# Seven more products in seven parts in the second layer of a two-layer encoder trunk, and an earlier place for the sums that two of them read

## The chip, the cores and the metric

The kernel runs on one core of a Trainium2 chip. Its time is the device time of one execution in microseconds (us). On the core, TensorE (PE in the profile) multiplies matrices, VectorE (DVE), ScalarE (ACT) and GpSimd (POOL) work element by element, SyncE (SP) issues transfers, and 16 DMA engines carry them out. TensorE writes into eight banks of PSUM.

## What is computed

The trunk has two layers over 512 frames of width 1024, in float32. The reference, cut to what the change touches:

```python
for i in range(DEPTH):
    h = rmsnorm(x, norm1_g[i])
    z = h @ w_in[i] + b_in[i]
    _, _, mv, mo, mi, mf, rq, rk, rv, rg, gm, gr = split_cols(z)
    ...
    hm = from_chunks(hm)                       # matrix memory, 4 heads of 256
    y_m = (jax.nn.sigmoid(mo) * head_layernorm(hm, m_norm_g[i], M_HEADS))
    ...                                        # retention gives y_r
    merged = jax.nn.sigmoid(gm) * (y_m @ w_bm[i]) + jax.nn.sigmoid(gr) * (y_r @ w_br[i])
    x = x + merged @ w_out[i]

    h2 = rmsnorm(x, norm2_g[i])
    x = x + jnp.square(jax.nn.relu(h2 @ w_ff1[i] + b_ff1[i])) @ w_ff2[i] + b_ff2[i]
    ...
```

`mo` has 1024 columns, 256 for each of four heads; its sigmoid is the output gate of the matrix memory. `w_ff1` is 1024 x 4096, `w_ff2` 4096 x 1024: the two products of the channel mix.

## The kernel before

**Float32 by three products.** Every operand is split into a high part, rounded to the matmul's float32r, and a low part, the rest. `split` (L302) makes both: ScalarE copies the high part (L303), VectorE subtracts (L304). A product is high x high + high x low + low x high, so three matmuls for each block of 128 rows of the inner dimension.

**Units of weights.** The weights come as a list of units, made by `unit_list` (L171) in the order of use, and loaded through SP's queue by `fill_raws` (L397), at most four pieces ahead (`RAWS`) and one more in places. Each piece is split before use (`prep_next`, L425). Three kinds matter here:

- a `T8` unit is 1024 x 128 of weights, one piece. `t8` (L484) makes 24 matmuls of 512 columns into one bank.
- a `PAIR` unit gives two such tiles, 256 columns, in seven products instead of eight (Strassen's scheme in Winograd's form): `run_pair` (L512), with 12 matmuls of 256 columns for each of seven parts, 84 in all, where two `T8` units have 48 of 512. The weights are pieces A, B, C (1024 wide) and D (512 wide), seven blocks of 128 x 512. The order of parts is P1, P5, P6, P2, P3, P7; P4 is put off (`later`) and made inside the next unit, after its first four inner blocks (`t8`, L491), after its P5 (`run_pair`) or after the first block of an attention (`attend`, L838), by `flush` (L507). Three banks hold the parts; ScalarE and VectorE gather them into two tiles y (`pair_tiles`, L587, ScalarE for P1, P5, P6, P4 and VectorE for P2, P3, P7). When P4 has come, `consume` goes on with the two tiles; the second comes with its sign turned.
- a `V` unit is a quarter of the weights of a value tile (`values`, L783).

**Sums.** A product in seven parts needs sums of blocks on both sides. The sums of weights (t1, t3, t2, t4) are made by DMA from DRAM to DRAM, some copying and some adding, on POOL's queue: `step` (L354) issues one, and holds it until the latest matmul has run. For groups that `is_full` (L128) names, all four are made so, in eight steps for a product; for others VectorE forms the rest. `tick` and `pace` (L365, L369) say when: each unit adds credit by its time in `TIME`, times `SHARE`, or `LATER` from a unit in the first layer on, less what its loads cost; a step takes `STEP` of credit. The order of steps is that of `groups` (L147), and a load of a group may only be issued when its steps are (the assertion in `fill_raws`). The sums of activations are made by VectorE and ScalarE: `xs_sums` (L1228), four calls of eight VectorE and two ScalarE instructions for the normed input x of the layer, and `n2_sums` (L1457) for the channel mix. They use scratch tiles of 128 x 512 (`tmp`, six of them in this stage, `NTMP`).

**Order around the change.** In the stage of the matrix memory the program runs, for heads 0 to 3, the query and key tiles (`m_qk`), scores, attention (`m_attend`), the gates (`m_gates`, two `T8` units a head) and the way back to the transposed form (`m_back`, transposes on TensorE and a gating on VectorE). The values of heads two and three are made by `mv_vals(1, ...)`, four `V` units; a function `mid` given to it runs ahead of its third unit. A scheduler then puts the instructions of each engine in an order of its own, by their place in the program and the tiles they need; the order shown in the profile is its outcome.

In the channel mix `ff_order` (L79) gives the sequence: the tiles (0,0) to (0,3) of the first product (256 hidden columns each, `ff1`, L1477), then for each b from 0 to 2 the tile (b+1,0), four output products (b,0) to (b,3) (`ff2`, L1514, always in seven parts), and the tiles (b+1,1) to (b+1,3); then the last four output products. An output product (b,p) reads the four hidden tiles (b,0) to (b,3). After each hidden tile come the norm's factor (L1485), relu and square on ScalarE, then the hidden tile's own split and sums for the next product (`pair_quarters`, `pair_operand`). `FPAIRS` (L90) lists the (b,p) that are made by `PAIR` units, five in each layer.

The instructions' names in the profile: l1f13 is layer two's hidden tile (1,3), and its matmuls are l1f13a, b, c by bank when it is a product in seven parts and l1f when it is two plain tiles; l1o10 is the output product (1,0); l1hh and l1hl are the hidden operands' high and low parts; l1m2o is the output gate of head three (counted from nought, 2), l1bgm a branch gate, l1xsh and l1xsl the sums of normed x, wh and wl the weights' parts (with a letter for pieces of a `PAIR`), s29t a sum of weights.

Of the kernel before, what the change touches and what calls it, by code (L numbers as in the profile page):

```python
# [37 lines left out]
AF = mybir.ActivationFunctionType  # L38
# [23 lines left out]
SIGN = (1.0, -1.0)  # L62
# [24 lines left out]

FPAIRS = ((1, 1), (1, 3), (2, 1), (2, 3), (3, 1))  # L90


PRODUCTS = {"P1": ("A", 0, 0), "P5": ("A", 1, 4), "P2": ("B", 0, 2), "P6": ("B", 1, 5), "P3": ("C", 0, 6),
# [14 lines left out]
HALVES = [(WIDE[x][0], u) for x, u in TURNS]  # L108

SOON = ("w_in", 0, CGM + 2 * P)  # L110
STEP, SHARE, LATER = 1.13, 0.75, 0.73
TIME = {"PAIR": (9.9, 3.9), "WIDE": (5.45, 2.7), "FULL": (9.9, 5.0)}


# [12 lines left out]

def is_full(g):  # L128

    return is_gate(g) or g[0] > 0 and g[1][0] == "f"  # L130


def has_t2(g):
# [4 lines left out]
def is_gate(g):  # L138
    return g[1][:2] == "rw"
# [7 lines left out]
def groups():  # L147


    g = {}  # L150
    for i in range(L):
        def rqk(h):
            return [("w_in", 0, c + k * 256) for k in (h, h + 1) for c in (CRQ, CRK)]

        g[i, "rv0"] = [("w_in", 0, CRV)]
        g[i, "rqk0"] = rqk(0)
        g[i, "gm"] = [("w_in", 0, CGM + 256 * p) for p in (2, 3)]
        g[i, "rw0"] = [("w_in", 0, CRG)]
        g[i, "rv2"] = [("w_in", 0, CRV + 1024)]
        g[i, "rqk2"] = rqk(2)  # L160
        g[i, "rw2"] = [("w_in", 0, CRG + 1024)]
        g[i, "gr"] = [("w_in", 0, CGR + 256 * p) for p in range(4)]
        for b in range(4):
            f = [p for c, p in FPAIRS if c == b]
            if f:
                g[i, f"fp{b}"] = [("w_ff1", 0, b * 1024 + 256 * p) for p in f]
            g[i, f"ff{b}"] = [("w_ff2", b * 1024, 256 * p) for p in range(4)]
    return g


def unit_list(i):  # L171

    u = [("IF",)]

    def t8(w, col, row=0):
        u.append(("T8", w, row, col))

    def v(col):
        for k in range(4):
            u.append(("V", k, col))  # L180

    def pair(g, p):
        u.append(("PAIR", (i, g), p))

    def mqk(h):
        for d in range(2):
            t8("w_in", CQ + h * 256 + d * P)
        for d in range(2):
            t8("w_in", CK + h * 256 + d * P)

    def mo(h):
        for d in range(2):
            t8("w_in", CO + h * 256 + d * P)

    def rqk(h):
        for a in range(2):
            pair(f"rqk{h // 2 * 2}", h % 2 * 2 + a)

    def full(w, col=0, row=0, lo=0, hi=8):
        for c in range(lo, hi):  # L200
            t8(w, col + c * P, row)

    mqk(0)
    v(CV)
    full("w_in", CGM, 0, 0, 2)
    mqk(1)
    mo(0)
    full("w_in", CGM, 0, 2, 3)
    mqk(2)
    mo(1)  # L210
    v(CV + 512)
    mqk(3)
    mo(2)
    full("w_in", CGM, 0, 3, 4)
    mo(3)
    u.append(("WIDE", (i, "rv0"), 0))
    full("w_bm", 0, 0, 0, 4)
    rqk(0)
    for p in (2, 3):
        pair("gm", p - 2)  # L220
        full("w_bm", 0, 0, 2 * p, 2 * p + 2)
    rqk(1)
    u.append(("WIDE", (i, "rw0"), 0))
    u.append(("WIDE", (i, "rv2"), 0))
    rqk(2)
    full("w_br", 0, 0, 0, 4)
    rqk(3)
    full("w_br", 0, 0, 4, 8)
    u.append(("WIDE", (i, "rw2"), 0))
    for p in range(4):  # L230
        pair("gr", p)
        full("w_br", 0, 1024, 2 * p, 2 * p + 2)
    full("w_out")

    def pairs(seq):
        for kind, b, p in seq:
            if (b, p) in FPAIRS and kind == "f":
                pair(f"fp{b}", [q for c, q in FPAIRS if c == b].index(p))
            elif kind == "f":
                t8("w_ff1", b * 1024 + 256 * p)  # L240
                t8("w_ff1", b * 1024 + 256 * p + P)
            else:
                pair(f"ff{b}", p)

    pairs(ff_order()[0])
    u.append(("PE", 0))
    pairs(ff_order()[1])
    u.append(("PE", 1))
    full("w_pe_gate")
    return u  # L250


def build(ctx, tc, ins, out):
# [529 lines left out]
    def values(i, nm, act, rc, bv_ap, n_, mid=None):  # L783

        bvt = tmp(f"{nm}bv")
        (gp if nm == "l0m0" else nc.sync).dma_start(bvt, bv_ap)
        o = [ps(f"{nm}vp{j}") for j in range(NT)]
        for u in range(4):
            _, wh, wl = unit("V")
            if u == 1:  # L790
                flush()
            if u == 2 and mid:
                mid()
            for kk in range(2):
                k = 2 * u + kk
                s = slice(kk * T, (kk + 1) * T)
                for j in range(NT):
                    js = slice(j * P, (j + 1) * P)
                    te.matmul(o[j], act[0][k][:, js], wh[:, s], start=(k == 0), stop=False)
                    te.matmul(o[j], act[0][k][:, js], wl[:, s], start=False, stop=False)  # L800
                    cur["mm"] = te.matmul(o[j], act[1][k][:, js], wh[:, s], start=False, stop=(k == KT - 1))
                pace()
        vh = [cur["low"].tile([P, 576], F32R, name=f"{nm}vh{j}", tag="vh", bufs=NT) for j in range(NT)]
        vl = [cur["low"].tile([P, 576], F32R, name=f"{nm}vl{j}", tag="vl", bufs=NT) for j in range(NT)]
        for j in range(NT):
            rows_split_v(i, None, nm, n_, j, o[j], rc, bvt, vh[j], vl[j])
        return vh, vl
# [167 lines left out]
    for i in range(L):  # L975
# [125 lines left out]
        def m_gates(h, act, nrm):  # L1101
            return [gated(f"l{i}m{h}o{v}", t8(act, f"l{i}m{h}o{v}"), nrm, AF.Sigmoid, bcol(i, "bo", 2 * h + v))
                    for v in range(2)]

        def m_back(h, gs, num):
            gate_out(f"l{i}m{h}o", gs, num, [bcol(i, "gmn", 2 * h + v) for v in range(2)], ym, 2 * h)

# [129 lines left out]
        def mv_vals(pr, act, rc, mid=None):  # L1237
            return values(i, f"l{i}m{pr}", act, rc, bias_rows(pr * 512), 2, mid)
# [95 lines left out]
        xs_sums(0)  # L1334
        num = m_attend(1, pt, vv)
        gs = m_gates(1, xn, None)
        vv = mv_vals(1, xn, None, lambda: m_back(1, gs, num))
        xs_sums(1)
        pt = m_scores(2, qk)
        qk = m_qk(3, xn, None)  # L1340
        xs_sums(2)
        num = m_attend(2, pt, vv)
        gs = m_gates(2, xn, None)
        gm_tile(3, xn, None)
        m_back(2, gs, num)
        xs_sums(3)
        pt = m_scores(3, qk)
        gs = m_gates(3, xn, None)
        num = m_attend(3, pt, vv)
        vv = rv_vals(0, lambda: m_back(3, gs, num))  # L1350

# [125 lines left out]
        def ff1(b, p):  # L1477
# [8 lines left out]
                ac.activation(a, a, AF.Relu, bias=bcol(i, "bf1", 8 * b + 2 * p + d), scale=sign)  # L1486
                ac.activation(a, a, AF.Square)

            if (b, p) in FPAIRS:
                def consume(y):  # L1490
                    for d in range(2):
                        evac(d, y[d], SIGN[d])
                    pair_quarters(st, *hid[b, p])
                    pair_operand(nm, st, *hid[b, p])

                pair_tiles(nm, n2_seven, consume, [st[:, d * T:(d + 1) * T] for d in range(2)])
                return
# [303 lines left out]
```

## Time and profile before

| | us |
|---|---|
| median of three runs | 2322.41 |
| lowest and highest | 2320.74, 2324.77 |
| the profiled execution | 2324.59 |
| its span, first to last instruction | 2322.9 |
| VectorE busy | 1752.4 |
| ScalarE busy | 1257.8 |

The page of the profile has one execution. A row of a timeline gives the start of an instruction from the span's start, its duration, engine, line, operation, what it writes and reads, its shape, and in brackets the idle time of its engine just before it and what ended that. Matmuls overlap in their pipeline: the duration of 0.39 us for 512 columns contains the start of the next one, so what a matmul costs is read from start to start. A row of the windows gives, for a stretch, its length and then the busy time of PE, weight loads, DVE, ACT and POOL, each with its count, then the granted clock, the DMA engines' share and GB/s. In the table of waits a row has the waiting instruction, what released it, the total in us, the times and the longest.

### The profile page before, as it was taken

The page shows a single profiled execution, that of the slowest core. Times are in us where ns is not written, and L with a number is a line of the kernel's source. Part 1 is how long each engine was busy: PE and PEld are TensorE (multiplying, and loading weights), DVE is VectorE, ACT ScalarE, POOL GpSimd, SP SyncE. Part 2 cuts the span into 40 slices and gives each one's busy share as a digit, 9 for nine tenths or more (in the row PEclk, how much of TensorE's full clock was granted, in tenths as well). Part 3 has the DMA queues.
Part 4 walks back from the last instruction along what each step waited for, and adds up shares of the span by engine and source line. Part 5 has one row for each costly group of instructions (what it writes and reads, how often), then busy time and mean ns, then how long its engine had stood idle before and what let it go on. Part 6 is the DMA issues. An engine that isn't in the chain of part 4 may idle for free.

```text
span 2322.9 us, 35908 instructions
## 1 busy us (share of the span) xinstructions
PE 2306.3 (99%) x13352; PEld 2033.3 (88%) x13352; DVE 1752.4 (75%) x2665; ACT 1257.8 (54%) x1807; POOL 600.4 (26%) x944
## 2 busy tenths in 40 slices
PE   9999999999999999999999999999999999999998
PEld 8888889888898899999888888988888888999997
DVE  7878767886767878778778777778767677787785
ACT  6756544644554546546557564445445445456464
POOL 4333222223124322212533232221231242110012
PEclk9999999999999999999999999999999999999999
DMA  7776887787788788888777678877777887884541
GB/s 219 186 190 174 240 222 216 213 230 210 222 235 258 204 232 218 230 233 210 220 214 179 181 180 250 222 202 219 215 218 206 241 258 187 249 226 152 172 159 55
DMA packets 180799, 484.89 MB, mean 209 GB/s; under 512 B 25024, under 2 KB 28480, under 8 KB 180624
## 3 DMA queue, kind: packets, MB, share of 16 engines
q1 hardware_dynamic: 110896, 277.13, 35.8%
q0 software_dynamic: 54320, 178.04, 35.4%
q10 hardware_dynamic: 15408, 27.43, 3.4%
q8 instruction: 104, 1.70, 0.3%
q14 instruction: 71, 0.58, 0.1%
HBM read 463.63 MB, written 184.03 MB: 279 GB/s over the span
## 4 chain that ended last, share of the span: by engine, by line
PE 90%; DVE 5%; issue 2%; DMA 1%; ACT 1%; POOL 1%; DVEq 0%; ACTq 0%; SPq 0%; POOLq 0%
PE l1f L480 2%; PE l1f L481 2%; PE l1f L482 2%; PE l0br L480 1%; PE l1br L480 1%; PE l1br L481 1%; PE l0br L481 1%; PE l1br L482 1%; PE l0br L482 1%; PE l0f L480 1%; PE l0f L481 1%; PE l0f L482 1%; PE l0pg L480 1%; PE l1bm L480 1%; PE l0bm L480 1%
## 5 line engine op out<-in xcount | busy, mean ns | idle before, releaser
L303 ACT ACTIVATE wh<-wr 128x1024 fp32r<-128x1024 f32 (+1 forms) x203 | 210.3, 1042 | 154.3 <-issue 22.1
L304 DVE TENSOR_TENSOR wl<-wr,wh 128x1024 fp32r<-128x1024 f32 (+1 forms) x201 | 245.6, 1224 | 38.5 <-ACT wh L303 38.3
L303 ACT ACTIVATE wh_B<-wr 128x1024 fp32r<-128x1024 f32 x118 | 125.0, 1059 | 187.6 <-PE l0br L481 15.7
L304 DVE TENSOR_TENSOR wl_B<-wr,wh_B 128x1024 fp32r<-128x1024 f32 x118 | 144.2, 1222 | 56.4 <-ACT wh_B L303 51.9
L303 ACT ACTIVATE wh_C<-wr 128x1024 fp32r<-128x1024 f32 x70 | 74.0, 1057 | 74.2 <-PE l0br L481 9.7
L304 DVE TENSOR_TENSOR wl_C<-wr,wh_C 128x1024 fp32r<-128x1024 f32 x70 | 85.5, 1222 | 22.1 <-ACT wh_C L303 21.3
L303 ACT ACTIVATE wh_D<-wr 128x512 fp32r<-128x512 f32 x70 | 44.1, 630 | 102.9 <-DVE wr L462 32.0
L303 ACT ACTIVATE wh_A<-wr 128x1024 fp32r<-128x1024 f32 x70 | 73.7, 1053 | 43.3 <-DMA wr<-wpairs 8.8
L303 ACT ACTIVATE wh_t<-wr 128x1024 fp32r<-128x1024 f32 x56 | 59.4, 1060 | 67.2 <-PE l1g2va L576 6.0
L304 DVE TENSOR_TENSOR wl_A<-wr,wh_A 128x1024 fp32r<-128x1024 f32 x70 | 85.5, 1221 | 10.4 <-ACT wh_A L303 9.9
L304 DVE TENSOR_TENSOR wl_t<-wr,wh_t 128x1024 fp32r<-128x1024 f32 x56 | 68.2, 1221 | 26.2 <-ACT wh_t L303 25.6
L480 PE MATMUL l1f<-l1n2h,wh 128*128 128x512 f32 x176 | 68.7, 390 | 0.0
L480 PE MATMUL l0f<-l0n2h,wh 128*128 128x512 f32 x176 | 68.7, 390 | 0.0
L481 PE MATMUL l0f<-l0n2l,wh 128*128 128x512 f32 x176 | 68.6, 390 | 0.0
L481 PE MATMUL l1f<-l1n2l,wh 128*128 128x512 f32 x176 | 68.6, 390 | 0.0
L482 PE MATMUL l0f<-l0n2h,wl 128*128 128x512 f32 x176 | 68.5, 389 | 0.0
L482 PE MATMUL l1f<-l1n2h,wl 128*128 128x512 f32 x176 | 68.5, 389 | 0.0
L304 DVE TENSOR_TENSOR wl_D<-wr,wh_D 128x512 fp32r<-128x512 f32 x70 | 48.3, 690 | 26.2 <-ACT wh_D L303 24.4
L695 POOL TENSOR_TENSOR l1n3sum<-l1n3sum,l1n3sq 128x512 f32<-128x512 f32 x6 | 8.2, 1367 | 166.4 <-ACT l1n3sum L687 143.8
L482 PEld LDWEIGHTS l0f<-l0n2h,wl 128*128 128x128 f32 x176 | 33.0, 188 | 7.0
L482 PEld LDWEIGHTS l1f<-l1n2h,wl 128*128 128x128 f32 x176 | 33.0, 188 | 7.0
L480 PEld LDWEIGHTS l0f<-l0n2h,wh 128*128 128x128 f32 x176 | 33.1, 188 | 6.6
(5550 smaller groups left out, 8953.2 us busy)
## 6 DMA issues: line engine op xcount, KB each, us to landing
wr<-wstream SPq DMA_DIRECT2D x199, 512.0 KB, 4.9
wr<-wpairs SPq DMA_DIRECT2D x210, 256.0 KB, 3.9
wr<-wwide SPq DMA_DIRECT2D x48, 512.0 KB, 4.8
s3t<-wwide POOLq DMA_DIRECT2D x24, 256.0 KB, 5.0
s6t<-wwide POOLq DMA_DIRECT2D x24, 256.0 KB, 5.3
s18t<-wwide POOLq DMA_DIRECT2D x24, 256.0 KB, 5.3
s21t<-wwide POOLq DMA_DIRECT2D x24, 256.0 KB, 4.4
s23t<-wpairs POOLq DMA_DIRECT2D x24, 256.0 KB, 5.0
```

Source lines behind the costliest of these rows:

```text
L303: a = ac.activation(hi_ap, src, AF.Copy)
L304: return a, ve.tensor_sub(lo_ap, src, hi_ap.bitcast(F32))
L480: te.matmul(o, sh, mh, start=first, stop=False)
L481: te.matmul(o, sh, ml, start=False, stop=False)
L482: cur["mm"] = te.matmul(o, sl, mh, start=False, stop=last)
L695: (add or gp).tensor_tensor(self.sum, self.sum, sq, OP.add)
```

## The change

Ten tiles of the second layer's first channel-mix product are made by `PAIR` units instead of five; the first layer keeps its five. The output gates of heads 2 and 3 of the second layer become two `PAIR` units, with sums of weights of their own (`is_full` names them), and a function `m_pair` that puts the sigmoid on the two gathered tiles. Since these read the sums of normed x, all four `xs_sums` calls stand ahead of `m_scores(2)`: the second and third inside `mid` of the values of heads two and three, behind `m_back(1)`, and the fourth behind those values. `mid` runs one `V` unit sooner. The order of sums holds in both layers. `LATER` goes from 0.73 to 0.77, from a unit late in the first layer's retention on.

```diff
-FPAIRS = ((1, 1), (1, 3), (2, 1), (2, 3), (3, 1))
+FPAIRS = (((1, 1), (1, 3), (2, 1), (2, 3), (3, 1)), ((0, 2), (1, 0), (1, 1), (1, 3), (2, 0), (2, 1), (2, 3), (3, 0), (3, 1), (3, 2)))
+MPAIRS = (1,)
...
-STEP, SHARE, LATER = 1.13, 0.75, 0.73
+STEP, SHARE, LATER = 1.13, 0.75, 0.77
...
-    return is_gate(g) or g[0] > 0 and g[1][0] == "f"
+    return is_gate(g) or g[0] > 0 and g[1][0] in "fm"
...
+        if i in MPAIRS:
+            g[i, "mo"] = [("w_in", 0, CO + 256 * h) for h in (2, 3)]
...
-    mo(2)
+    pair("mo", 0) if i in MPAIRS else mo(2)
     full("w_in", CGM, 0, 3, 4)
-    mo(3)
+    pair("mo", 1) if i in MPAIRS else mo(3)
...
-            if u == 2 and mid:
+            if u == 1 and mid:
                 mid()
...
+        def m_pair(h):
+            gs = []
+
+            def consume(y):
+                for v in range(2):
+                    ac.activation(y[v], y[v], AF.Sigmoid, bias=bcol(i, "bo", 2 * h + v), scale=SIGN[v])
+                    gs.append(y[v])
+
+            pair_tiles(f"l{i}m{h}o", xs, consume)
+            return gs
...
-        vv = mv_vals(1, xn, None, lambda: m_back(1, gs, num))
-        xs_sums(1)
+        def between():
+            m_back(1, gs, num)
+            xs_sums(1)
+            xs_sums(2)
+
+        vv = mv_vals(1, xn, None, between)
+        xs_sums(3)
         pt = m_scores(2, qk)
         qk = m_qk(3, xn, None)
-        xs_sums(2)
         num = m_attend(2, pt, vv)
-        gs = m_gates(2, xn, None)
+        gs = m_pair(2) if i in MPAIRS else m_gates(2, xn, None)
         gm_tile(3, xn, None)
         m_back(2, gs, num)
-        xs_sums(3)
         pt = m_scores(3, qk)
-        gs = m_gates(3, xn, None)
+        gs = m_pair(3) if i in MPAIRS else m_gates(3, xn, None)
         num = m_attend(3, pt, vv)
         vv = rv_vals(0, lambda: m_back(3, gs, num))
...
-            if (b, p) in FPAIRS:
+            if (b, p) in FPAIRS[i]:
```

More of the change, by code (lines that the diff above doesn't have):

```diff
@@ L163, in groups @@
         for b in range(4):
-            f = [p for c, p in FPAIRS if c == b]
+            f = [p for c, p in FPAIRS[i] if c == b]
             if f:
@@ L236, in pairs @@
         for kind, b, p in seq:
-            if (b, p) in FPAIRS and kind == "f":
-                pair(f"fp{b}", [q for c, q in FPAIRS if c == b].index(p))
+            if (b, p) in FPAIRS[i] and kind == "f":
+                pair(f"fp{b}", [q for c, q in FPAIRS[i] if c == b].index(p))
             elif kind == "f":
```

## The prediction

> **What bounds the kernel now.** I read the page first: span, busy shares, granted clock, DMA.
>
> ```profile
> span 2322.9 us, 35908 instructions
> PE 2306.3 (99%) x13352; PEld 2033.3 (88%) x13352; DVE 1752.4 (75%) x2665; ACT 1257.8 (54%) x1807; POOL 600.4 (26%) x944
> PEclk9999999999999999999999999999999999999999
> DMA  7776887787788788888777678877777887884541
> ```
>
> TensorE is busy 99% of the span at full clock in every slice. Because modelled ends hide short stalls, I went on to the table of who waited for whom, TensorE alone:
>
> ```profile
> PE l1r0brqa L531 <- DVE l1r0brqy L612: 1.7, 1, 1.7
> ```
>
> This is its longest wait, in the second layer, where the change is. So a change pays by the matmul stream that it shortens, and loses by a wait that it puts into that stream. The price of both must come from start to start, not from the modelled durations. The timeline of TensorE around the second layer's product (1,3), the four-operand tile that follows it, and the first output product:
>
> ```profile
> 2037.07 0.28 PE L531 MATMUL l1f13a<-l1n2h,wh_A 128*128 128x256 f32 x1
> ...
> 2045.70 0.40 PE L480 MATMUL l1f<-l1n2h,wh 128*128 128x512 f32 x1
> ...
> 2048.45 0.28 PE L531 MATMUL l1f13a<-l1n2h,wh_D 128*128 128x256 f32 x1
> ...
> 2049.88 0.40 PE L480 MATMUL l1f<-l1n2h,wh 128*128 128x512 f32 x1
> ...
> 2058.07 0.28 PE L531 MATMUL l1o10a<-l1hh,wh_A 128*128 128x256 f32 x1
> ...
> 2060.66 0.28 PE L532 MATMUL l1o10c<-l1hl,wh_A 128*128 128x256 f32 x1
> ...
> 2060.90 0.28 PE L531 MATMUL l1o10b<-l1hh,wh_B 128*128 128x256 f32 x1
> 2061.08 0.38 PE L531 MATMUL l1o10a<-l1hh,wh_B 128*128 128x256 f32 x1
> 2061.30 0.28 PE L532 MATMUL l1o10a<-l1hl,wh_B 128*128 128x256 f32 x1
> ```
>
> A product in seven parts costs 8.63 us for six of them (2037.07 to 2045.70, 1.44 each) and 1.43 us for the seventh, which runs inside the next unit (2048.45 to 2049.88): **10.06 us**. The same 256 columns as two plain tiles, unit (2,0), cost 2.75 us before that insert and 8.19 us after it: **10.94 us**. The difference is 0.88 us.
>
> **The change part by part.**
>
> *Five more products in layer two's first channel mix* ((0,2), (1,0), (2,0), (3,0), (3,2); the other five of the ten are there already): 5 x 0.88 = 4.40 us less matmul time.
>
> *The output gates of heads three and four in layer two.* Now each is two plain tiles, between these starts:
>
> ```profile
> 1359.31 0.40 PE L480 MATMUL l1m2o<-l1xnh,wh 128*128 128x512 f32 x1
> ...
> 1370.22 0.39 PE L480 MATMUL l1bgm<-l1xnh,wh 128*128 128x512 f32 x1
> ```
>
> That is 10.91 us. The nearest product on the same input is the branch gate's:
>
> ```profile
> 1500.20 0.28 PE L531 MATMUL l1bgm3a<-l1xnh,wh_A 128*128 128x256 f32 x1
> ...
> 1508.74 0.40 PE L480 MATMUL l1bm<-l1ymh,wh 128*128 128x512 f32 x1
> ...
> 1511.50 0.28 PE L531 MATMUL l1bgm3a<-l1xnh,wh_D 128*128 128x256 f32 x1
> ...
> 1512.93 0.40 PE L480 MATMUL l1bm<-l1ymh,wh 128*128 128x512 f32 x1
> ```
>
> 8.54 + 1.43 = 9.97 us, so 0.94 less, twice: 1.88 us. The stream gets 4.40 + 1.88 = **6.28 us** shorter. The Trainium skill (TensorE: Matmul & The Clock Gate, Back-to-back issue gap) gives 262 cycles for 256 columns and 518 for 512 at 2.4 GHz; by that a product is 84 x 0.109 = 9.2 us, two tiles 48 x 0.216 = 10.4 us, and the sum an estimated 7 x 1.2 = 8.4 us. The rows show both forms slower, and the short form more so; the sum above goes by the rows.
>
> *VectorE and ScalarE.* A product splits three and a half weight pieces where two tiles split two. By the rows of VectorE further below a piece costs it 1.13 us from start to start (2046.94 to 2048.07) and an eviction of a part 0.33 (2046.61 to 2046.94; three of seven are VectorE's): 1.5 pieces and three evictions make about +2.7 us of VectorE, and I take as much for ScalarE. Windows of the stages:
>
> ```profile
> 1329.50:1359.30 29.80, 29.80 (x152) 25.52 (x152) 26.28 (x49) 21.77 (x40) 7.53 (x13) 1.00 0.60 156
> 2014.60:2058.00 43.40, 43.40 (x278) 39.60 (x277) 29.85 (x42) 28.70 (x40) 8.88 (x13) 1.00 0.84 213
> 2065.40:2094.90 29.50, 29.50 (x252) 29.50 (x251) 22.23 (x36) 11.60 (x13) 4.16 (x6) 1.00 0.86 240
> ```
>
> The third figure is VectorE. In the channel mix it has 29.85 of 43.40 us (69%); one more product there makes 32.6 of 42.5 (77%). On average that is hidden; the order is not, as follows.
>
> *Where it is late next.* After product (1,3) come (2,0) and then output product (1,0), which needs the hidden tile of (1,3) in its fourth piece. The same holds for (2,3), (3,0) and (2,0). VectorE around it:
>
> ```profile
> 2046.61 0.42 DVE L612 TENSOR_TENSOR l1f13st<-l1f13a,l1f13st 128x256 f32<-128x256 f32 x1
> 2046.94 1.22 DVE L304 TENSOR_TENSOR wl_A<-wr,wh_A 128x1024 fp32r<-128x1024 f32 x1
> 2048.07 0.69 DVE L1485 TENSOR_TENSOR l1f13st<-l1f13st,l1n2rb 128x512 f32<-128x512 f32 x1
> ...
> 2053.26 0.68 DVE L1485 TENSOR_TENSOR l1f20st<-l1f,l1n2rb 128x512 f32<-128x512 f32 x1
> ...
> 2055.06 1.22 DVE L304 TENSOR_TENSOR wl_C<-wr,wh_C 128x1024 fp32r<-128x1024 f32 x1
> ...
> 2057.74 1.23 DVE L304 TENSOR_TENSOR l1hl<-l1f13st,l1hh 128x1024 fp32r<-128x1024 f32 x1 [1.13 <-ACT l1hh L303]
> ```
>
> The seventh part of (1,3) ends at 2049.88; its last operand (l1hl) is there at 2058.97, 9.09 us later. TensorE wants it at 2060.66, so there are 1.7 us to spare. When (2,0) is a product too, the seventh part is followed by four parts of it (5.76 us) and, 2.59 us into the output product, by the matmul that wants the operand: 8.35 us. As the chain runs now it would be 0.74 us late. Lower bound: without the two foreign instructions in the chain (0.6 and 1.13) it takes 7.36 us and nothing waits, even the existing slips are saved. Those are the steps of 0.18 and 0.22 at 2060.90 and 2061.08 where 0.12 is usual, 0.16 us. Upper bound: three evictions of (2,0) and one more weight piece go in between, 9.09 + 1.0 + 1.13 = 11.2, 2.9 us late. Behind the waiting matmul stand the rest of the output product and the seventh part of (2,0), which needs only its own evictions and could be put ahead: the rows at 2060.90 and 2061.08 show the order on TensorE already crossing from part to part. The nearest row for such a crowded place is the first layer's, where VectorE forms sums of weights besides:
>
> ```profile
> 910.02 0.28 PE L533 MATMUL l0o10c<-l0hh,wl_A 128*128 128x256 f32 x1
> 910.41 0.36 PE L531 MATMUL l0o10a<-l0hh,wh_B 128*128 128x256 f32 x1
> ...
> 913.68 0.28 PE L532 MATMUL l0o11c<-l0hl,wh_A 128*128 128x256 f32 x1
> 914.08 0.38 PE L531 MATMUL l0o10c<-l0hh,wh_C 128*128 128x256 f32 x1
> ```
>
> 0.39 and 0.40 instead of 0.12: 0.55 us at one output product. I take that, less the 0.16 already paid, at both places: **+0.8 us**; range -0.3 to +5.5.
>
> *Sums of normed x sooner, back-transform one unit sooner (both layers).* The gate products read all four sums, from about 1360.8 (second part, 1.44 us after 1359.31); now the last is written late:
>
> ```profile
> 1306.77 1.39 DVE L853 TENSOR_SCALAR l1m1num<-l1m1num,l1m1mv,l1m1hv 128x256 f32<-128x256 f32 x4 [1.50 <-POOL l1m1hv L1097]
> ...
> 1313.28 1.23 DVE L304 TENSOR_TENSOR wl<-wr,wh 128x1024 fp32r<-128x1024 f32 x1 [4.00 <-ACT wh L303]
> 1318.30 0.75 DVE L873 SCALAR_TENSOR_TENSOR l1m1o0g<-l1m1ot,bc,l1m1o0g 128x512 f32<-128x512 f32 x1 [3.79 <-PE l1m1ot L859]
> ...
> 1383.89 0.69 DVE L304 TENSOR_TENSOR l1xsl<-l1xs3u,l1xsh 128x512 fp32r<-128x512 f32 x1 [0.50 <-ACT l1xsh L303]
> ```
>
> The transposes move one value unit up (24 matmuls, 5.4 us), to about 1312.2; what they read is there at 1308.16. VectorE sits idle there for 4.0 and 3.8 us before two of its instructions; two of the sums (some 5 us each) go in there, and the third leaves the windows of attention two and three. Cost nothing; without that cover, 26.28 of 29.80 us in the window before attention two say that 5 us more would stall TensorE by 1 to 2 us.
>
> *Sums of weights.* Seven groups of eight steps, 56 on top of 630, each 0.26 MB on POOL's queue, and 0.79 MB more of loads per product (seven of 0.26 MB for two of 0.52): 20 MB on the 485 of the whole run, 4%. Now the last of them:
>
> ```profile
> L361 POOL DMA_DIRECT2D s29t<-wpairs x24: 506/788/804, 1974.1 to 2088.6; - x24
> ...
> DMA to landing us min/median/max: 2.7/4.8/9.1
> ```
>
> 0.79 us of POOL each, 44 us on an engine that is 26% busy; the masks of scores three stand behind steps on POOL, and gain the 5 us that the fourth sum leaves. The pace goes from 0.73 to 0.77. Counted in credits through the unit list, the last group is complete about 46 us before its first use, where the least in the old first layer is 39; a step lands within 9.1. Nothing on the path.
>
> **Sum:** -6.28 + 0.8 = -5.5 us. The profiled execution took 2324.59 us (span 2322.9 and 1.7 around it), so 2319.1; it lies 2.2 above the median of the runs, 2322.41, against which the forecast is **2316.9 us**.
>
> **Rivals.**
> (A) *The operand chain takes the place of the matmuls saved*: both places at their upper bound, 2 x (2.9 - 0.16) = 5.5: 2322.41 - 6.28 + 5.5 = **2321.6**, no difference. For it: VectorE would have two products in a row, each close to 9.9 us of work in 10.06 (22.23 x 9.9 / 29.5 = 7.5 for an output product, plus evaluation and operands, some 2.4). Against it: the order of TensorE can cross parts.
> (B) *Transfers become the bound, slower.* Place: second layer from (1,0) to (3,2), 21 products with only two plain pairs between them. Each product moves 1.84 MB of loads and, at the new pace, 2.3 steps of 0.26: 2.44 MB in 10.06 us, 243 GB/s. It decides once the DMA share reaches 1, that is once the engines give less than 243. At 0.6 us late per product, 21 x 0.6 - 6.28 = +6.3: **2328.7**. Against it: the window at 2065.40 moves 240 GB/s at a share of 0.86 with no stall, so full share is 279. The Trainium skill (DMA: Bandwidth & Descriptors, Where 436 GB/s comes from) states that about 358 GB/s of HBM is one core's limit; with steps read and written I estimate 304 here, so by that rule B does not come.
> (C) *The sums of normed x are late for the first gate product*: the bias rows keep one of six scratch tiles, and a sum waits for it past 1331. Some 4 us at one place: 2322.41 - 5.5 + 4 = **2320.9**. Against it: some 30 us remain.
>
> **How the numbers follow.** Forecast 0.55, A 0.27, B 0.13, C 0.05. A measurement tells some 0.2%, 4.6 us, from no change: 2317.8 to 2327.1 is the same. The forecast is only 0.9 us beyond that edge, but its chain may also come out cheaper; of its 0.55 I put 0.47 on faster and 0.08 on same, of A 0.03 faster, 0.22 same, 0.02 slower, C is same, B slower: 0.50, 0.35, 0.15. Range: from all stalls gone and the runs' spread of 2 us (2314.6) to A and C with that spread (2324.5); B is left out.
>
> **What would show it.** Product (2,0) of layer two at about 10.06 us from start to start, gate product of head three at 9.97; on TensorE before output products (1,0) and (2,0), steps of 0.1 to 0.6 us; the last l1xsl before 1350; no wait of TensorE behind a DMA; DMA share in 2100 to 2170 up from about 0.5 to 0.8. Wrong: waits of 1 us and more at the output products (A), ScalarE or VectorE waiting for loads of weights (B), TensorE idle at l1m2o (C), or products that cost more than 10.5 us.

## The result, and the profile after

| | before | after |
|---|---|---|
| median of 20 runs each, side by side (us) | 2322.51 | 2318.61 |
| lowest and highest | 2319.29, 2326.03 | 2316.68, 2321.94 |
| the profiled execution | 2324.59 | 2321.67 |
| its span | 2322.9 | 2320.0 |
| matmuls | 13352 | 13604 |

The ratio is 0.9985, with a 95% interval of 0.9979 to 0.9992: 3.5 us faster, by less than the 0.2% that the prediction took as its bound. The forecast was 2316.9. The page of the changed kernel:

```profile
span 2320.0 us, 36685 instructions
PE 2302.4 (99%) x13604; PEld 2041.1 (88%) x13604; DVE 1771.8 (76%) x2700; ACT 1275.9 (55%) x1849; POOL 633.8 (27%) x1000
DMA  6777787777789888888886778877877898888751
```

252 matmuls more (seven products of 84 for seven pairs of 48), VectorE 19.4 us and ScalarE 18.1 us busier, 2.8 and 2.6 for each product. In the DMA slices the rise is near the end. TensorE's timeline around layer two's (2,0), now a product, and at the gate of head three:

```profile
2044.05 0.28 PE L536 MATMUL l1f20a<-l1n2h,wh_A 128*128 128x256 f32 x1
...
2046.93 0.28 PE L536 MATMUL l1f13a<-l1n2h,wh_D 128*128 128x256 f32 x1
...
2048.37 0.28 PE L536 MATMUL l1f20a<-l1nsh,wh_B 128*128 128x256 f32 x1
...
2054.13 0.28 PE L536 MATMUL l1o10a<-l1hh,wh_A 128*128 128x256 f32 x1
...
2056.61 0.29 PE L536 MATMUL l1f20a<-l1n2h,wh_D 128*128 128x256 f32 x1
...
2058.05 0.28 PE L536 MATMUL l1o10a<-l1hh,wh_B 128*128 128x256 f32 x1
```

```profile
1361.68 0.28 PE L536 MATMUL l1m2oa<-l1xnh,wh_A 128*128 128x256 f32 x1
...
1370.23 0.40 PE L485 MATMUL l1bgm<-l1xnh,wh 128*128 128x512 f32 x1
...
1372.98 0.28 PE L536 MATMUL l1m2oa<-l1xnh,wh_D 128*128 128x256 f32 x1
...
1374.41 0.40 PE L485 MATMUL l1bgm<-l1xnh,wh 128*128 128x512 f32 x1
```

(2,0) takes 2.88 us before the inserted seventh part of (1,3), 5.76 after it and 1.44 for its own seventh: 10.08. The gate takes 8.55 + 1.43 = 9.98 us. Summed from start to start over all matmuls that changed form, channel mix and gates take 5.86 us less (4.07 and 1.79). The span fell by 2.9. So about 3 us were given back, and the table of waits, TensorE alone, shows some places:

```profile
PE l0gr0a L536 <- ACT l0gr0y L607: 0.8, 1, 0.8
...
PE l1o20a L537 <- DVE l1hl L309: 0.4, 1, 0.4
...
PE l1o20c L536 <- ACT l1hh L308: 0.2, 1, 0.2
PE l1o01a L536 <- DVE l1x L1540: 0.2, 1, 0.2
```

The first row lies in the first layer, where no product was added. To catch the short ones too, I summed for each kernel by how much TensorE's steps, from the start of one matmul to the start of the next, exceed the usual one of their form (226.7 ns for 512 columns, 117.8 for 256, the median for other forms; steps within 8 ns of it left out). This sum is called the excess below: 31.0 us before, 33.7 after. 5.86 less 2.7 is 3.2, near the span's 2.9.

### The profile page after: what moved, and what is told of

Same layout as the page of the kernel before. It is cut to its first block, busy times and chain, and to the rows that moved or that the text cites. A ratio compares the mean times of both kernels' runs of the same rounds, so it can differ in the third digit from the quotient of the medians.

```text
span 2320.0 us, 36685 instructions
## 1 busy us (share of the span) xinstructions
PE 2302.4 (99%) x13604; PEld 2041.1 (88%) x13604; DVE 1771.8 (76%) x2700; ACT 1275.9 (55%) x1849; POOL 633.8 (27%) x1000
## 4 chain that ended last, share of the span: by engine, by line
PE 89%; DVE 5%; DMA 2%; ACT 2%; issue 1%; POOL 0%; DVEq 0%; ACTq 0%; SPq 0%; POOLq 0%
PE l0br L485 1%; PE l1br L485 1%; PE l0br L486 1%; PE l1br L487 1%; PE l0br L487 1%; PE l1br L486 1%; PE l0f L485 1%; PE l0f L486 1%; PE l0f L487 1%; PE l1f L485 1%; PE l1f L486 1%; PE l1f L487 1%; DVE wl_B L309 1%; PE l0pg L485 1%; PE l0bm L485 1%
## 5 line engine op out<-in xcount | busy, mean ns | idle before, releaser
L308 ACT ACTIVATE wh<-wr 128x1024 fp32r<-128x1024 f32 (+1 forms) x189 | 195.4, 1041 | 121.8 <-issue 17.3
L309 DVE TENSOR_TENSOR wl<-wr,wh 128x1024 fp32r<-128x1024 f32 (+1 forms) x187 | 229.8, 1231 | 28.2 <-ACT wh L308 27.7
L309 DVE TENSOR_TENSOR wl_B<-wr,wh_B 128x1024 fp32r<-128x1024 f32 x125 | 152.8, 1223 | 58.3 <-ACT wh_B L308 53.6
L309 DVE TENSOR_TENSOR wl_C<-wr,wh_C 128x1024 fp32r<-128x1024 f32 x77 | 94.1, 1223 | 19.1 <-ACT wh_C L308 18.3
L309 DVE TENSOR_TENSOR wl_A<-wr,wh_A 128x1024 fp32r<-128x1024 f32 x77 | 94.0, 1221 | 12.5 <-ACT wh_A L308 11.2
L366 POOL DMA_DIRECT2D s31t<-wpairs x24 | 16.9, 705 | 84.0 <-PE l1o11a L538 9.7
L486 PEld LDWEIGHTS l0f<-l0n2l,wh 128*128 128x128 f32 x176 | 33.1, 188 | 6.4
L485 PE MATMUL l1f<-l1n2h,wh 128*128 128x512 f32 x96 | 37.6, 392 | 0.0
L486 PE MATMUL l1f<-l1n2l,wh 128*128 128x512 f32 x96 | 37.5, 391 | 0.0
L487 PE MATMUL l1f<-l1n2h,wl 128*128 128x512 f32 x96 | 37.4, 390 | 0.0
```

Of the source, the lines that this page charges most:

```text
L308: a = ac.activation(hi_ap, src, AF.Copy)
L309: return a, ve.tensor_sub(lo_ap, src, hi_ap.bitcast(F32))
L366: dma = gp.dma_start(piece(g, x, p, q), piece(g, MADE[x][a], p, q), max_dma_last_dim=4096, **kw)
L485: te.matmul(o, sh, mh, start=first, stop=False)
L486: te.matmul(o, sh, ml, start=False, stop=False)
L487: cur["mm"] = te.matmul(o, sl, mh, start=False, stop=last)
```

## The experiments

All with five rounds, the kernel before run beside them. In the text "+x us" is the ratio less 1, times 2322.9; an interval is about 0.0009 to either side, 2 us.

**The change taken apart.** *e1_moves*: the changed kernel without any new product: the sums and the back-transform moved, the pace at 0.77.

```diff
-FPAIRS = (..., ((0, 2), (1, 0), (1, 1), (1, 3), (2, 0), (2, 1), (2, 3), (3, 0), (3, 1), (3, 2)))
+FPAIRS = (..., ((1, 1), (1, 3), (2, 1), (2, 3), (3, 1)))
-MPAIRS = (1,)
+MPAIRS = ()
```

> The change without its products: the earlier sums of normed x, the earlier back-transform and the pace of 0.77 alone, five channel-mix products and plain gate tiles as before. Theory M (the gain is the shorter matmul stream less new stalls at places that the products crowd): no difference, within 1 us of the kernel before, and no place in the trace more than 0.3 us longer that is not also longer in another execution. Theory P (the earlier sums and the faster pace cost what is missing between 5.8 us of matmuls saved and 3.9 measured): 1.5 to 2 us slower than before.

Measured: 2327.02, ratio 1.0017 [1.0008, 1.0025], **+3.9 us** [1.9, 5.8], theory P and more. What the prediction had priced at nothing costs, by the middle of that interval, two thirds of what the products save. The trace agrees: its excess is 35.0 us, 4.0 more than before. The largest single place is the first values of layer two's retention. VectorE, then TensorE:

```profile
1402.38 1.22 DVE L471 TENSOR_TENSOR t<-wr,wr 128x1024 f32<-128x1024 f32 x1 [4.19 <-DMA wr<-wwide]
...
1404.82 1.22 DVE L309 TENSOR_TENSOR wl_t<-wr,wh_t 128x1024 fp32r<-128x1024 f32 x1
```

```profile
1406.09 0.50 PE L581 MATMUL l1r0vc<-wl_t,l1xsh 128*128 128x512 f32 x1 [1.25 <-DVE wl_t L309]
```

VectorE's sum waits 4.19 us for a load, the split behind it is late, and TensorE waits for that. In the kernel before the same sum does not wait:

```profile
1405.98 1.22 DVE L466 TENSOR_TENSOR t<-wr,wr 128x1024 f32<-128x1024 f32 x1
```

*e2_heads* adds the two gate products to this (new gates, old channel mix), *e3_ff* the five products of the channel mix (`MPAIRS = ()`), *e4_no_adjacent* is the changed kernel less the products (2,0) and (3,0), those that stand between another product and the output product that reads it.

```diff
 e2_heads, against the changed kernel:
-FPAIRS = (..., ((0, 2), (1, 0), (1, 1), (1, 3), (2, 0), (2, 1), (2, 3), (3, 0), (3, 1), (3, 2)))
+FPAIRS = (..., ((1, 1), (1, 3), (2, 1), (2, 3), (3, 1)))
 e3_ff:
-MPAIRS = (1,)
+MPAIRS = ()
 e4_no_adjacent:
-FPAIRS = (..., ((0, 2), (1, 0), (1, 1), (1, 3), (2, 0), (2, 1), (2, 3), (3, 0), (3, 1), (3, 2)))
+FPAIRS = (..., ((0, 2), (1, 0), (1, 1), (1, 3), (2, 1), (2, 3), (3, 1), (3, 2)))
```

> The two gate products alone, with the earlier sums and the pace; channel mix as before. Theory M: 1.8 us of matmuls saved, 0.8 of them given back in attention four of layer two (4.3 us there instead of 3.56), so 1.0 us faster than before. Theory P: 0 to 1 us slower than before; attention at 3.6.

Measured: 2323.94, ratio 1.0001 [0.9992, 1.0010]: the time of theory P, with the longer attention four of theory M (0.74 us of excess at l1m3a).

> The five further channel-mix products alone, with the earlier sums and the pace; gates as plain tiles. Theory M: 4.0 us of matmuls saved, 1 to 2 given back around the output products of layer two, so 2 to 3 us faster than before; attention four at 3.56 us. Rival H (the operand chain is hidden altogether): 4.0 us faster and no output product above 10.0 us.

Measured: 2324.93, ratio 1.0009 [1.0000, 1.0018]: 2 us slower than before, where theory and rival both had it faster. Neither counted the cost of moves and pace.

> The change without the channel-mix products (2,0) and (3,0), the two that stand between a product and the output products that need it. Theory M: 1.6 us of matmuls come back, and the stalls at output products (1,0), (1,2), (2,0), (2,2) go (1.5 us in the profile of the changed kernel), so within 0.5 us of the changed kernel, 3.5 to 4 faster than before. Rival H: 1.6 us slower than the changed kernel, 2.3 faster than before.

Measured: 2321.15, ratio 0.9989 [0.9981, 0.9998]: 2.6 us faster than before, close to rival H, and within the error of theory M too.

Against e1_moves the gates bring 3.7 us, the channel mix 1.9, both together 7.4, each with an error of 2.5 to 3 us. By the times alone the 3.7 can't be told from the gates' 1.79 of matmuls, but the traces show one thing more that the gates bring: with them, the wait at l1r0vc shown above is gone (0.2 us of excess at that tile in the changed kernel, 1.7 in e1_moves; in e3_ff, without the gates, TensorE again waits 1.7 there). So 5.86 + 1.5 = 7.4 us from the products, less 3.9 for moves and pace: the 3.5 measured. This sum takes in one place alone; over all tiles the excess falls from 35.0 to 33.7 us, so 1.3, which gives nearly the same. The two adjacent products bring 0.9 us in the ratios, too little to tell from nothing or from the 1.6 that their matmuls save.

**Pace or order?** *e7_pace* is the kernel before with the pace alone, *e8_order* with the moves alone.

```diff
 e7_pace, against the kernel before:
-STEP, SHARE, LATER = 1.13, 0.75, 0.73
+STEP, SHARE, LATER = 1.13, 0.75, 0.77
 e8_order, against e1_moves:
-STEP, SHARE, LATER = 1.13, 0.75, 0.77
+STEP, SHARE, LATER = 1.13, 0.75, 0.73
```

> The kernel before with the pace of the weight sums at 0.77 instead of 0.73 and nothing else. The moves and this pace together, without any new product, took 4.1 us more than the kernel before (ratio 1.0017). If the pace is what costs (theory Q: steps that are issued sooner fall on loads and on VectorE's and POOL's work, first of all in the first layer's retention gate and at the second layer's first retention values), this kernel takes 2325.5 to 2327 us, ratio 1.0012 to 1.0018, and the stalls at the first layer's gate part l0gr0c (about +1 us) and at l1r0vc (about +1.5) are in its trace. If the order is what costs (theory O), it takes 2322 to 2323.5 and both places look as before.

Measured: 2326.49, ratio 1.0013 [1.0004, 1.0022], **+3.0 us**, with the stall at l0gr0c (1.6 us of excess) but none at l1r0vc (0.2).

> The kernel before with the moves alone: sums of normed x sooner and the back-transform of head two one value unit sooner, in both layers, pace 0.73, no new product. Theory O (the order costs: transposes and sums one unit sooner make TensorE wait at the head of the matrix memory and what follows): 2326 to 2327.5 us, ratio 1.0013 to 1.002. Theory Q (the pace costs): 2322 to 2323.5, ratio 1.0000 +- 0.0005. If each brings half, both kernels lie near 2324.5 and 2325, and the two add up.

Measured: 2324.82, ratio 1.0004 [0.9995, 1.0013], +0.9 us, not to be told from nothing; l0gr0c as before. The two add up to e1_moves. The pace alone costs time by more than the error; for the moves alone that is not shown. That the pace costs more than the moves is not shown either: the difference, 2.1 us, has an error of 3. How the pace comes to TensorE can be followed in e7_pace at the first layer's retention gate. First GpSimd, VectorE, ScalarE and TensorE of e7_pace, then GpSimd and VectorE of the kernel before:

```profile
611.02 0.80 POOL L361 DMA_DIRECT2D s8t<-wpairs  x1 [10.63 <-PE l0g2va L577]
613.89 0.80 POOL L361 DMA_DIRECT2D s8t<-wpairs  x1 [2.07 <-PE l0g2vb L577]
616.52 0.54 POOL L361 DMA_DIRECT2D s8t<-wpairs  x1 [1.83 <-PE l0g2va L577]
```

```profile
621.37 0.69 DVE L459 TENSOR_TENSOR wr<-wr,wr 128x512 f32<-128x512 f32 x1 [2.34 <-DMA wr<-wpairs]
```

```profile
640.13 0.72 ACT L1191 ACTIVATE l0g2y<-l0g2y,l0r3hv 128x512 f32<-128x512 f32 x1 [1.88 <-POOL l0r3hv L1149]
...
643.03 0.36 ACT L602 ACTIVATE l0gr0y<-l0gr0a 128x256 f32<-128x256 f32 x1
```

```profile
643.45 0.39 PE L531 MATMUL l0gr0a<-l0xsh,wh_B 128*128 128x256 f32 x1 [1.36 <-ACT l0gr0y L602]
```

```profile
611.99 0.80 POOL L361 DMA_DIRECT2D s8t<-wpairs  x1 [7.84 <-PE l0g2va L577]
617.66 0.80 POOL L361 DMA_DIRECT2D s8t<-wpairs  x1 [4.87 <-PE l0g2va L577]
```

```profile
619.93 0.68 DVE L459 TENSOR_TENSOR wr<-wr,wr 128x512 f32<-128x512 f32 x1
```

Three sums of weights are issued within 5.5 us where there were two. VectorE's sum of two loaded pieces, which ran without a wait, now waits 2.34 us for its load; everything behind it on VectorE is late, and 22 us on ScalarE's eviction of the gate's first part, queued behind four instructions of the norm of retention head four, comes at 643.03. TensorE needs that bank for its third part and has waited 1.36 us. VectorE and ScalarE run their queues strictly in order by the Trainium skill (Perfetto Trace Analysis, Tensor Engine Instruction); these rows agree, with the eviction 2.5 us behind its matmuls (done by 640.51). It isn't that the transfers were full (e7_pace, then before):

```profile
600.00:640.00 40.00, 39.67 (x184) 32.52 (x184) 31.27 (x40) 23.05 (x32) 4.54 (x8) 1.00 0.65 192
```

```profile
600.00:640.00 40.00, 40.00 (x186) 32.92 (x185) 31.84 (x42) 24.33 (x34) 5.26 (x11) 1.00 0.65 193
```

Both have the same share, 0.65, over this stretch. All fourteen traces together, the wait of that one VectorE instruction and of that one matmul (us):

| kernel | pace in layer one | VectorE's wait | TensorE's wait |
|---|---|---|---|
| before, e8_order, e9_pace_two | 0.73 | 0, 0, 0 | 0, 0, 0 |
| e11_all_three | 0.73 | 0.27 | 0 |
| e6_hold | 0.77 | 0.67 | 0.28 |
| e10_order_two, e12_hold_order | 0.77 | 0.99, 1.02 | 0.59, 0.62 |
| the changed kernel | 0.77 | 1.24 | 0.85 |
| e5_priority, e3_ff, e2_heads | 0.77 | 1.31, 1.32, 1.33 | 0.94, 0.92, 0.93 |
| e1_moves | 0.77 | 1.49 | 1.07 |
| e4_no_adjacent, e7_pace | 0.77 | 2.14, 2.34 | 1.37, 1.36 |

TensorE's wait follows VectorE's, less 0.4 us of slack (0.8 to 1.0 in the last row). VectorE's comes with the pace of 0.77, but from 0.67 to 2.34 us at the same pace. In layer two the same instruction waits 2.49 us in e9_pace_two and 2.06 in e11_all_three, which have 0.79 there, and not at all in the other twelve, with 0.73 or 0.77. What these twelve waits of 0.67 us and more have in common, in 28 cases, is one sum of weights issued 5.1 to 5.3 us before VectorE is ready for the instruction (at 613.89 in e7_pace), as the middle one of three; the sixteen cases without it wait 0 to 0.27. This points to the moment at which a sum falls beside the loads, which the pace shifts, and not to the pace as such; no run moved that one sum alone.

This is one path, and not the whole. The same trace of e7_pace has two of the kernel's longest waits shortened. The one at l1r0brqa, 1.7 us before, the prediction shows; the other of before, then both in e7_pace:

```profile
PE l0r0brqa L531 <- DVE l0r0brqy L612: 1.6, 1, 1.6
```

```profile
PE l0r0brqa L531 <- DVE l0r0brqy L612: 0.6, 1, 0.6
PE l1r0brqa L531 <- DVE l1r0brqy L612: 0.5, 1, 0.5
```

Over all tiles its excess is only 1.0 us above before (32.0 and 31.0). Where the 3.0 us of its runs go, the trace does not show.

**Two stalls that the trace of the changed kernel shows.** *e5_priority* puts what follows a hidden product ahead of the splits of weights:

```diff
 def consume(y):
-    for d in range(2):
-        evac(d, y[d], SIGN[d])
-    ...
+    with ahead():
+        for d in range(2):
+            evac(d, y[d], SIGN[d])
+        ...
```

> The changed kernel with one edit: everything that follows a hidden product (factor, relu and square, sums, operand split) is put ahead of the splits of weights in the scheduler's order. In the changed kernel the last operand of hidden tile (1,3) and of (2,3) is written some 11.7 us after the seventh part, behind three splits of weights, and TensorE loses about 0.9 us at output product (2,0) and 0.5 at output (0,1). Theory: the operands come some 3 us sooner, these two stalls go, and the kernel takes 1.0 to 1.5 us less than the changed one (2317 to 2317.8). Rival: the splits of weights are now late for the parts of the next product instead, a wait of TensorE for wh or wl letters of 0.3 us and more at several products, and it takes as much as the changed kernel or more (2318.6 to 2322).

Measured: 2326.90, ratio 1.0017 [1.0008, 1.0026], +3.9 us, so 7 us worse than the changed kernel. The last operand of (1,3) did come sooner, started at 2055.85 where the changed kernel has 2059.05. Then ScalarE and TensorE:

```profile
2066.65 1.06 ACT L308 ACTIVATE wh_C<-wr 128x1024 fp32r<-128x1024 f32 x1 [4.05 <-DMA wr<-s27t]
...
2069.80 1.06 ACT L308 ACTIVATE l1hh<-l1f20st 128x1024 fp32r<-128x1024 f32 x1 [1.36 <-DVE l1f20st L628]
2070.77 1.04 ACT L308 ACTIVATE wh_B<-wr 128x1024 fp32r<-128x1024 f32 x1
```

```profile
2071.86 0.58 PE L536 MATMUL l1o11b<-l1hh,wh_B 128*128 128x256 f32 x1 [3.35 <-ACT wh_B L308]
```

ScalarE's queue stops for a load, an operand and its wait stand ahead of the next piece's split, and TensorE waits 3.35 us for that. The excess in the channel mix rose from 3.6 us in the changed kernel to 11.8. The rival came, larger than it was put: the splits ahead of the operand are what keep the weights on time.

*e6_hold* issues no sum of weights from head four's gate product to the end of its attention:

```diff
-        if at["step"] < len(steps) and at["credit"] >= 0:
+        if at["step"] < len(steps) and at["credit"] >= 0 and not cur.get("hold"):
...
+        cur["hold"] = i in MPAIRS
         gs = m_pair(3) if i in MPAIRS else m_gates(3, xn, None)
         num = m_attend(3, pt, vv)
+        cur["hold"] = False
```

> The changed kernel with one edit: no sum of weights is issued between the gate product of head four and the end of its attention in layer two, so that the masks on GpSimd do not stand behind a step that waits for the gate product's matmuls. Theory: the stall at attention four's first tile l1m3a (4.33 us where it was 3.56) goes back to 3.6, and the kernel takes 0.7 us less than the changed one (about 2318). Rival: the masks wait for something else (scores from TensorE or their own chain on VectorE and ScalarE), l1m3a stays above 4.2, and the time stays at 2318.6. A second way to lose: the steps held back are crowded behind the attention and cost more than 0.7 there.

Measured: 2319.80, ratio 0.9985 [0.9976, 0.9993], as the changed kernel. GpSimd in the changed kernel, then in e6_hold:

```profile
1384.57 0.52 POOL L366 DMA_DIRECT2D s22t<-s22t  x1 [0.65 <-PE l1m3oa L538]
1385.95 0.50 POOL L366 DMA_DIRECT2D s22t<-s22t  x1 [0.85 <-PE l1m3oc L538]
1386.45 0.30 POOL L1082 TENSOR_SCALAR_AFFINE_SELECT l1m3D<-l1m3D 128x128 f32<-128x128 f32 x1
```

```profile
1381.34 0.29 POOL L1082 TENSOR_SCALAR_AFFINE_SELECT l1m3D<-l1m3D 128x128 f32<-128x128 f32 x1 [8.70 <-ACT l1m3D L1077]
1384.04 0.61 POOL L1082 TENSOR_SCALAR_AFFINE_SELECT l1m3D<-l1m3D 128x128 f32<-128x128 f32 x1 [2.41 <-ACT l1m3D L1077]
```

The second mask comes at 1386.45 behind two steps that wait for the gate's own matmuls, and at 1384.04 without them. The stall of the attention went as expected (0.75 us of excess to 0.01); the time of the whole shows nothing of it, and 0.7 us is less than these runs can tell.

**Versions that might be better.** *e9_pace_two*: the changed kernel with 0.73 through layer one and 0.79 from layer two on. *e10_order_two*: with the old order of sums and back-transform in layer one. *e11_all_three*: both, and the hold. *e12_hold_order*: the hold and the old order in layer one, pace 0.77 as changed.

```diff
-(SHARE if at["unit"] <= rush else LATER)
+(SHARE if at["unit"] <= rush else EARLY if at["unit"] <= layer2 else LATER)
```

For the old order in layer one:

```diff
-            if u == 1 and mid:
+            if u == (1 if i in MPAIRS else 2) and mid:
...
-        xs_sums(3)
+        xs_sums(3 if i in MPAIRS else 1)
...
+        if i not in MPAIRS:
+            xs_sums(2)
```

> The changed kernel with the faster pace of the weight sums in layer two alone: 0.73 as before up to the end of layer one, 0.79 from there (enough for the groups of the new products). The kernel before with pace 0.77 throughout was at ratio 1.0013 and stalled 1.6 us at the first layer's retention gate (l0gr0c). Theory (the pace costs in layer one, where no new product needs it): l0gr0c goes back to 0.1 us, and the kernel takes 1 to 2.5 us less than the changed one, ratio 0.9975 to 0.9980. Rival (the pace costs where the transfers are densest, in layer two): 0.79 there makes it worse, ratio 0.9985 to 0.9995, even if l0gr0c is mended.

Measured: 2321.98, ratio 0.9994 [0.9985, 1.0002]: no gain, a loss of about 2 us against the changed kernel. The stall at l0gr0c is gone, and its twin is in layer two (VectorE, then the table of waits):

```profile
1775.09 0.69 DVE L465 TENSOR_TENSOR wr<-wr,wr 128x512 f32<-128x512 f32 x1 [2.49 <-DMA wr<-wpairs]
```

```profile
PE l1gr0a L537 <- ACT l1gr0y L608: 1.3, 1, 1.3
```

> The changed kernel with the old order of sums and of the back-transform in layer one, where no gate product needs the new one; layer two as in the changed kernel. The moves alone in both layers were at ratio 1.0004, some +1 us. Theory (half of that is layer one's, and its first retention values l0r0vc, 0.56 us of stall in the changed kernel, 0.11 before, are part of it): l0r0vc back near 0.1, 0.5 us less than the changed kernel, ratio 0.9983, which the runs can hardly tell from 0.9985. Rival: l0r0vc stays, since it comes with the pace, and the time is the changed kernel's or worse by the 1 us that the old order lost at l0r0brkc (1.80 before, 0.82 after).

Measured: 2319.15, ratio 0.9983 [0.9975, 0.9992]. l0r0vc is back at 0.12 us of excess, and l0r0brkc at 1.97: both sides of the expectation came in the trace, 0.4 us less and 1.2 more; the time can't be told from the changed kernel's.

> The changed kernel with three edits: faster pace in layer two alone (0.73, then 0.79), old order of sums and back-transform in layer one, and no sum of weights issued between the gate product of head four and the end of its attention in layer two. If the three add as their stalls in the traces do (1.0 at l0gr0c, 0.45 at l0r0vc, 0.75 at l1m3a, less 1.0 at l0r0brkc), 1.2 to 2 us less than the changed kernel, ratio 0.9977 to 0.9980. If nothing of them can be measured: 0.9985 +- 0.0007.

Measured: 2321.48, ratio 0.9991 [0.9982, 1.0000]. Again l1gr0a waits 1.4 us, behind a load wait of 2.06 on VectorE.

> The changed kernel with two edits: no sum of weights issued between the gate product of head four and the end of its attention in layer two, and the old order of sums and back-transform in layer one; pace 0.77 as in the changed kernel. Each alone was within the noise of the changed kernel (0.9985 and 0.9983). With both and the pace of 0.79 in layer two the ratio was 0.9991. If that loss is the pace's (theory Q), this one is at 0.9977 to 0.9985, the lowest of the study, and l1gr0c has no stall. If the two edits do not add, or hurt together, it is at 0.9988 to 0.9994 like that kernel, and the pace in layer two was not what cost.

Measured: 2317.73, ratio 0.9979 [0.9970, 0.9988], the lowest of the study, 4.9 us below the kernel before. It differs from e11_all_three by the pace alone (0.77 against 0.73, then 0.79), and l1gr0c has no stall. Twice the pace of 0.73 and then 0.79 cost 2 to 3 us (0.9994 against 0.9985, 0.9991 against 0.9979); each pair's intervals overlap, so the size is not sharp, but both point one way. No kernel was run with 0.73 in layer one and 0.77 in layer two, so what the pace costs in layer one by itself stays open. That e12_hold_order beats the changed kernel is not shown: 0.9979 and 0.9985 lie within each other's intervals.

## Why the prediction was right in its direction and too large in its size

*What bounds it, and the matmuls saved.* Right. 6.28 us were predicted, 5.86 came: a product cost 10.08 where 10.06 was read, and the two-tile form it replaced 10.89 on average where one place read 10.94. The gates: 1.79 for 1.88.

*VectorE and ScalarE.* 2.7 us a product was predicted for each; 2.8 and 2.6 came.

*The operand behind the hidden product.* The step named the right wait and place, and its reading of the chain was off. VectorE of the changed kernel at (2,3), and three matmuls from the output product (2,0):

```profile
2136.06 0.95 DVE L309 TENSOR_TENSOR l1hl<-l1f23st,l1hh 128x768 fp32r<-128x768 f32 x1
...
2137.85 1.22 DVE L309 TENSOR_TENSOR wl_B<-wr,wh_B 128x1024 fp32r<-128x1024 f32 x1
...
2141.20 1.23 DVE L309 TENSOR_TENSOR l1hl<-l1f23st,l1hh 128x1024 fp32r<-128x1024 f32 x1 [0.52 <-ACT l1hh L308]
```

```profile
2136.38 0.28 PE L536 MATMUL l1o20a<-l1hh,wh_A 128*128 128x256 f32 x1
2137.06 0.39 PE L537 MATMUL l1o20a<-l1hl,wh_A 128*128 128x256 f32 x1 [0.41 <-DVE l1hl L309]
...
2138.46 0.29 PE L536 MATMUL l1f30a<-l1n2h,wh_D 128*128 128x256 f32 x1
```

The seventh part of (2,3) ends at 2129.55, its last operand is written at 2142.43: 12.9 us, beyond the upper bound of 11.2 (11.9 at (1,3), 2048.37 to 2060.28). TensorE's order is the same at both places. The seventh part of the next hidden product runs in the middle of the output product, as `run_pair` has it after P5 (2056.61 to 2058.05 in l1o10, 2138.46 to 2139.91 in l1o20), and the matmul that wants the last operand starts at 2060.47 and 2142.63: 12.1 and 13.1 us after the seventh part, where the prediction counted 8.35. So rival A's premise came, a late operand, and its price did not. What differs between the places is VectorE, about 1 us later at (2,0): the first part of the low operand, written from 2136.06 on, is wanted before it is there (the 0.41 us above), while at (1,0) it is there 0.5 us early. In excess, TensorE lost 0.9 us more than before at (2,0) and nothing at (1,0), and 0.5 us appeared at output product (0,1): 0.8 us predicted for two places, about 1.4 at two, of which only one is a predicted place. Why VectorE is later at (2,0) was not followed; in the other six kernels with all seven products the excess at that place lies between 0.07 and 0.86 us.

*Sums of normed x and the back-transform, "cost nothing".* The last instruction of the sums starts at 1340.02, before the 1350 that was named, and the gate product of head three waits for none, so rival C did not come. e8_order puts the price of the moves at 0.9 +- 2 us: nothing is not refuted.

*Sums of weights, "nothing on the path".* **This is the step that failed.** It asked only whether each group would be ready before its first use, and it was. It did not ask whom the sooner steps would delay. e7_pace prices that at +3.0 us [0.9, 5.1]; one path that the traces show, 1.4 us in e7_pace and 0.85 in the changed kernel, is the chain from a late load through VectorE and ScalarE. The rest is not placed. The share of the step on the masks, which "gain the 5 us that the fourth sum leaves", went the other way too: TensorE now begins attention four in the middle of the gate product (1386.8; before, at 1392.0, behind it), and the masks behind the steps on GpSimd were late for that (0.75 us; e6_hold removes it).

*Rival B.* The share of the DMA engines rose as told, before and after, and TensorE waited for no transfer directly:

```profile
2100.00:2180.00 80.00, 80.00 (x586) 75.92 (x585) 60.12 (x90) 45.77 (x59) 0.00 (x0) 1.00 0.51 160
```

```profile
2100.00:2180.00 80.00, 79.43 (x620) 76.98 (x619) 62.47 (x93) 47.22 (x66) 11.24 (x17) 1.00 0.81 233
```

The rival looked for lost bandwidth in the stage with the products. The sign that the prediction gave for it, VectorE waiting for loads of weights, did come, but elsewhere: what transfers cost in the chain above was the lateness of single loads, in a stage at a share of 0.65.

*What was missed in the sum, with the other sign.* The gate products also removed a wait of 1.5 us that moves and pace alone made at l1r0vc. Put together: -5.86 for the matmuls, -1.5 at l1r0vc, +3.9 for moves and pace gives the 3.5 us measured; the 0.75 at the masks and the 1.4 at the output products lie within the error of that sum. The forecast's 5.5 was 2 us too much, and the result is on the "same" side of its 0.2%, which had 0.35. That it was not further off is partly luck: the two terms that the prediction lacked have opposite signs.

*The range.* Its ends do not follow from the terms that it names. All stalls gone and 2 us of spread give 2322.41 - 6.28 - 0.3 - 2 = 2313.8 and not 2314.6; A and C together with that spread give 2321.6 + 4 + 2 = 2327.6 and not 2324.5. The measured 2318.61 lies within both.

## What to carry to other kernels

Work that only has to be done in time isn't free when it is done sooner: in a kernel that splits and sums each weight on engines with strict queues, one load that lands 2 us late is still there 20 us on, as an eviction that comes late. Price a change of pace where its transfers meet loads, not at its deadline, and take the change apart into its saving and its preparations, since here the preparations cost some two thirds of the saving. An operand that looks late in the trace may be late for a reason: look at what stands ahead of it before giving it priority.

## What the hardware showed that I had not expected

The same matmul has more than one pace. Twelve matmuls of 256 columns of output product (2,1) take, between these starts, 1.36 us in e1_moves and 1.41 in e7_pace:

```profile
2150.81 0.28 PE L536 MATMUL l1o21a<-l1hh,wh_A 128*128 128x256 f32 x1
...
2152.17 0.28 PE L536 MATMUL l1o21c<-l1hh,wh_A 128*128 128x256 f32 x1
```

```profile
2150.20 0.28 PE L531 MATMUL l1o21a<-l1hh,wh_A 128*128 128x256 f32 x1
...
2151.61 0.28 PE L531 MATMUL l1o21c<-l1hh,wh_A 128*128 128x256 f32 x1
```

That is 113.3 against 117.5 ns at full granted clock; the hidden products above step at 120 (1.44 us for 12). The faster step comes for whole stretches of 20 to 30 us of output products, in other places in each trace: about 1190 such steps in e1_moves, 1020 in e2_heads, 620 in e6_hold, 130 to 480 in the other kernels but e8_order (590). A thousand of them are worth some 4.2 us, more than the change. So a single profiled span (e1_moves: 2322.5, the kernel before: 2322.9) can hide what the medians show (+3.9 us). The five profiled executions with the most such steps (e1_moves, e2_heads, e6_hold, e8_order, e11_all_three) lie 1.2 to 2.6 us below the median of their own kernel, and the other nine 0.3 below to 4.9 above: this looks like a property of the execution and not of the kernel. What sets it was not found. By the Trainium skill (TensorE: Matmul & The Clock Gate, Back-to-back issue gap) the gap of a single matmul of 256 columns, taken alone, is 262 cycles, 109 ns at 2.4 GHz; no twelve in a row came to that here (113.2 at the least).
